# A gated linear attention layer on one Trainium2 core: the scores of each level as pairs of 64 by 64 blocks on the two column halves of TensorE

## The chip, the cores and the metric

The kernel runs on one core of a Trainium2 chip. The metric is the time of one execution in microseconds (us) on the device. Engines are named as the profile names them: PE is TensorE's matmul, PEld its weight load (it overlaps PE), DVE is VectorE, ACT is ScalarE, POOL is GpSimd, SP is SyncE, which issues the DMAs.

## What is computed

One layer of a diffusion backbone: a modulated norm, one input projection of 1024 channels, a bidirectional gated linear attention (4 heads, keys of 128, values of 256), a pooling mixer, two branch projections, a merge by gates, an output projection with residual and final norm, over 1024 latent tokens (256 context tokens give the first states). The part that the change touches is the score term of the attention, in the reference:

```python
diff = b[:, :, :, None, :] - b[:, :, None, :, :]
decay = jnp.exp(jnp.where(tri[:, :, None], diff, -jnp.inf))
scores = jnp.einsum('bhid,bhjd,bhijd->bhij', qc, kc, decay)
o = jnp.einsum('bhij,bhjv->bhiv', scores, vc) + jnp.einsum(
    'bhid,bhdv->bhiv', qc * jnp.exp(b), S)
```

Query i and key j of one chunk meet with a decay per channel, the product of the gates of the tokens between them. Both directions are summed, so a chunk's score matrix A is full, not triangular.

## The kernel before

Inputs, weights and results are float32. The projections split each operand into two float32r parts and add three products (tiles `wh`/`wl` are the parts of a weight, `h` those of the normed input, `ppj` is their PSUM bank, 512 or 256 columns at a time). Attention's own products are plain float32 matmuls, and each of these appears in the trace as two MATMUL records and two weight loads.

The heads run one after the other (`gla(h, ...)`, then `gates`, `head_k`, `head_q` and `head_v` of head h + 1). A head has two halves of 512 tokens, each with four chunks of 128. `head_scores` builds a half's scores in seven levels, for blocks of 1, 2, 4, .. 64 tokens: at a level, each block meets its sibling in a pair of blocks. For a level, `level_scores` multiplies, chunk by chunk, the keys of 128 tokens (`k`, the stationary operand) with the queries of 128 tokens (`level(q, hl)`, the moving one) into the PSUM tile `psc`, and one predicated copy on DVE takes from it, under the level's mask `msk`, what belongs to that level into `A`. Then `double_k` and `double_q` multiply keys (`s2`, `qk`) and queries (the tile `z`, called `qd` in the code) by decays, in place for the queries, which makes them the operands of the next level. So a level is a loop: matmuls, masked copy, decay of queries, matmuls. There are 4 heads x 2 halves x 7 levels = 56 calls.

A tile framework puts the program into an order for each engine ahead of time, by priorities and a cost model, so between the levels' matmuls PE's queue holds projections of the next head or of the pooling branch, and the queue is worked off in that order. In `gates`, matmuls read 64 partitions each (rows 0 to 63 or 64 to 127 of the array; tile `lr`). At the program's start, the modulation vectors are products whose result is 4 rows high (128 x 4 stationary, tiles `sil` and `cs`), which lie on a 32-column strip of the array.

Line numbers: L77 is the helper `mm`, L66 is `tt`, L63 is `act`, L487 the masked copy.

Of the kernel before, what the change touches and what calls it, by code (L numbers as in the profile page):

```python
# [15 lines left out]
P = 128  # L16
# [6 lines left out]
CPH = HALF // P  # L23
# [11 lines left out]

# slots of the one SBUF pool, by tag; PSUM banks, by tag
BUFS = dict(h=32, wr=2, wh=4, wl=4, z=2, t8=1, lr=5, s2=8, sw=2, v=8, qk=8, bx=1, A=2, kt=2, S=6, S0=4, on=1,
# [5 lines left out]
def hybrid_kernel(ctx: ExitStack, tc: tile.TileContext, x, ctx_in, rows, w_mod, b_gate_row,  # L43
# [38 lines left out]
    def split(hi, lo, src):  # L82
        """src = hi + lo, exactly, both float32r"""
        act(hi, src)
        tt(lo, src, hi.bitcast(F32), ALU.subtract)

    def chunks(ap, n=P):
        return ap.rearrange("p (c n) -> p c n", n=n)

    # ---- constants and small vectors as columns  # L90
    cst = const("cst", [P, N_CONST])
# [18 lines left out]

    # ---- token tiles: load, root mean square, normalise
    pow_in = const("pow_in", [P, 10])
# [21 lines left out]

    # ---- low-rank gate inputs, stacked parts on partitions
    def low_rank_weights():
# [16 lines left out]

    # ---- modulation: shift and scale as columns [d, (latent, context)]
    sA = const("sA", [P, KT, 2])
# [7 lines left out]
    def modulate(kt, t0, n, c, ptag):  # L163
        """psum of one row tile of xn^T and the scale and shift that make it h^T"""
        pt = PT(ptag)
        for i in range(n // P):
            nc.tensor.transpose(pt[:, i * P:(i + 1) * P],
                                xs[t0 + i][kt // 4][:, (kt % 4) * P:(kt % 4 + 1) * P], ident)
        return pt[:, :n], sA[:, kt, c:c + 1], shA[:, kt, c:c + 1]
# [71 lines left out]

    # ---- weight stream: slots of 1024 columns, split into exact float32r parts
    ahead = [False]

    def wslot(src, shape, col_scale=None):
        """rows [p, k, n] of a weight; per k: (hi, lo)"""
        _, nk, n = shape
        per = HALF // n
        parts = []
        with tc.high_priority() if ahead[0] else nullcontext():  # L250
            raw = T("wr", shape)
            load(raw, src)
            if col_scale is not None:
                tt(raw, raw, col_scale.rearrange("p (k n) -> p k n", k=1).to_broadcast(shape), ALU.mult)
            for k0 in range(0, nk, per):
                kn = min(per, nk - k0)
                hi, lo = T("wh", [P, kn, n], F32R), T("wl", [P, kn, n], F32R)
                split(hi, lo, raw[:, k0:k0 + kn, :])
                parts += [(hi[:, i, :], lo[:, i, :]) for i in range(kn)]
        return parts  # L260
# [4 lines left out]
    def wquad(w, c0, col_scale=None):  # L265
        """256 columns, all rows"""
        parts = []
        for kh in range(2):
            src = w[kh * HALF:(kh + 1) * HALF, c0:c0 + 256]
            parts += wslot(src.rearrange("(k p) n -> p k n", p=P), [P, 4, 256], col_scale)  # L270
        return parts

    def proj_t(w, rhs_hi, rhs_lo, n):
        """psum[128 columns, n tokens] = W^T h"""
        pt = PT("pj")
        nk = len(w)
        for k in range(nk):
            whi, wlo = w[k]
            mm(pt[:, :n], whi, rhs_hi[k], k == 0, False)
            mm(pt[:, :n], whi, rhs_lo[k], False, False)  # L280
            mm(pt[:, :n], wlo, rhs_hi[k], False, k == nk - 1)
        return pt

    def proj_n(w, lhs_hi, lhs_lo, tok):
        """psum[128 tokens, 256 columns] = h W"""
        pt = PT("pj")
        for k in range(KT):
            whi, wlo = w[k]
            mm(pt[:, :256], lhs_hi[k][:, tok], whi, k == 0, False)
            mm(pt[:, :256], lhs_hi[k][:, tok], wlo, False, False)  # L290
            mm(pt[:, :256], lhs_lo[k][:, tok], whi, False, k == KT - 1)
        return pt
# [25 lines left out]

    # ---- context: final states of both directions
    S0 = [None] * NH  # L320
# [28 lines left out]
    def transpose_k(src, tag):  # L349
        """four of [dk, 128] -> [token, chunk, dk]"""  # L350
        pt = PT("tr")
        for i in range(CPH):
            nc.tensor.transpose(pt[:, i * P:(i + 1) * P], src[i], ident)  # L353
        kT = T(tag, [P, CPH, P])
        act(kT, chunks(pt))
        return kT
# [32 lines left out]

    # ---- latent heads  # L390
    def rope_apply(pt, hf, scale):
# [37 lines left out]

    # Queries and keys lie with their two decays side by side: slot 1 is what a left block gives to the  # L430
    # scores with its right neighbour (backward decay of queries, forward of keys), slot 0 is for right blocks.
    # Decays of tokens and blocks: array 0 has the backward one of the even and the forward one of the odd,
    # array 1 the others.
    DEC_OFF = {2: 0, 4: 256, 8: 384, 16: 448, 32: 480, 64: 496, 128: 504}
# [8 lines left out]
    def level(t, hl):  # L443
        """slot 1 of the even blocks of hl tokens and slot 0 of the odd ones: [pair, block, token]"""
        t = t.rearrange("p n d -> p (n d)").rearrange("p (g x) -> p g x", x=4 * hl)[:, :, 1:4 * hl - 1]
        return t.rearrange("p g (s r) -> p g s r", s=2)[:, :, :, 0:2 * hl - 1:2]

    def gates(h):
        """per half: decays of the tokens, and of the blocks of 2, 4, .. 128 tokens"""
        both = T("bx", [P, 2, 2, HALF])  # L450
# [30 lines left out]
    def level_scores(hl, A, q, k):  # L481
        pl = PT("sc")
        n = P // (2 * hl)
        for c in range(CPH):
            mm(pl[:, c * P:(c + 1) * P], k[:, c * P:(c + 1) * P], level(q, hl)[:, c * n:(c + 1) * n], True, True)
        li = LEVELS.index(hl)
        nc.vector.copy_predicated(A, msk[:, li:li + 1, :].to_broadcast([P, CPH, P]), chunks(pl))  # L487

    def double_q(hl, t, dec):
        """from blocks of hl tokens to blocks of 2 hl"""  # L490
        t = level(t, hl)
        dec = dec.rearrange("p (g s n) -> p g s n", s=2, n=1)[:, :, ::-1, :]
        tt(t, t, dec.to_broadcast([P, HALF // (2 * hl), 2, hl]), ALU.mult)

    def double_k(hl, cur, rest, dec):
        """the same; cur meets its sibling in the scores of a level"""
        shape = [P, HALF // (4 * hl), 2, hl]
# [6 lines left out]
    def head_scores(h, st, decays):  # L504
        """per half: scores within chunks; queries and keys with the decay up to the ends of their chunk:
        qf, qb, kf, kb by chunk; and the decays of the chunks, forward and backward"""
        one, e = decays
# [78 lines left out]

    # ---- context states and latent heads
    msk_f = T("bx", [P, len(LEVELS), P])
# [33 lines left out]

    # ---- pooling branch
    def pool_gate(g):
# [26 lines left out]
    def pool_diff(g, u):  # L651
        """split tiles of (windowed mean - u)^T for one row tile"""
        w = WINDOWS[g]
# [44 lines left out]

    # ---- products of 2 x 2 blocks by seven block products (Winograd's form):
    #      row blocks m of W^T, inner blocks j (odd and even row tiles), token halves hf  # L700
    half_tile = {}

    def slot2(tag, dt=F32R):
        """two tiles of 512 columns"""
        if tag in ("t8", "bx"):
# [17 lines left out]
    def block_operands(o, val):  # L723
        """splits the operands of a row tile pair from the values of R11, R12, R22, R21 (overwritten)"""
        def put(n, v):
# [15 lines left out]
    def operands_h(g, tags, temps):  # L741
        """block operands of h^T, row tiles 2g and 2g + 1"""
        k0, k1 = 2 * g, 2 * g + 1
# [53 lines left out]
    def block_product(w, c0, ops, outs, post, by_rows=False, pre=None):  # L797
        """outs[m][hf] = (W^T X) of two column tiles from c0; post(m, hf) when one is done"""
        with tc.high_priority():
# [46 lines left out]

    # ---- pool groups; block operands of h^T meanwhile
    h_tags = {"T2": ["v"] * 4, "T3": ["lr", "lr", "S0", "S0"], "T1": ["S", "S", "S", "A"], "T4": ["bx", "bx", "kt", "sw"]}
# [53 lines left out]

    # ---- gates of the merge
    def release_order(tags):
# [37 lines left out]
    for i in range(2):  # L942
        for mp in range(4):
            if (i, mp) != (0, 0):
                gate_pair(i, mp)
            if (i, mp) == (1, 1):
                gb_ops.append(gb_operands(0))
    # ---- pool branch output
    gb_ops += [gb_operands(g) for g in range(1, 4)]
# [16 lines left out]

    # ---- attention branch output, merged
    freed = release_order(b_tags)
# [34 lines left out]

    # ---- output projection, residual and final norm
    mH = [[None] * KT for _ in range(2)]
# [107 lines left out]
```

## Time and profile before

| what | value |
|---|---|
| time, median of 3 runs | 1150.31 us (1150.07 to 1152.89) |
| span of the profiled execution | 1152.8 us |
| busy: PE, PEld, DVE, ACT | 1119.6, 926.7, 812.2, 493.4 us |
| chain that ended last: PE's share | 86% |
| TensorE clock granted from 58 us on (mean of the span 0.995) | 1.0 |

The profiled execution's span is the time of the slowest of the three runs less about 0.1 us. Busy times are the sum of an engine's records, and matmul records overlap, so a busy PE says that it was never long without work, not that it ran at its peak. Steps between starts say how long a matmul really holds the engine.

### The profile page before, as it was taken

The page shows a single profiled execution, that of the slowest core. Times are in us where ns is not written, and L with a number is a line of the kernel's source. Part 1 is how long each engine was busy: PE and PEld are TensorE (multiplying, and loading weights), DVE is VectorE, ACT ScalarE, POOL GpSimd, SP SyncE. Part 2 cuts the span into 40 slices and gives each one's busy share as a digit, 9 for nine tenths or more (in the row PEclk, how much of TensorE's full clock was granted, in tenths as well). Part 3 has the DMA queues.
Part 4 walks back from the last instruction along what each step waited for, and adds up shares of the span by engine and source line. Part 5 has one row for each costly group of instructions (what it writes and reads, how often), then busy time and mean ns, then how long its engine had stood idle before and what let it go on. Part 6 is the DMA issues. An engine that isn't in the chain of part 4 may idle for free.

```text
span 1152.8 us, 16292 instructions
## 1 busy us (share of the span) xinstructions
PE 1119.6 (97%) x5993; PEld 926.7 (80%) x5993; DVE 812.2 (70%) x1533; ACT 493.4 (43%) x962; POOL 24.2 (2%) x50
## 2 busy tenths in 40 slices
PE   6799999999999999999999999999999999999997
PEld 1268998798798798788888888888887886878997
DVE  4677458488588587698988867665768776757454
ACT  6697552462452552543333433343446324113233
POOL 0100000000000000100000000000000000000001
PEclk9899999999999999999999999999999999999999
DMA  8812150120220310103251463524448468982113
GB/s 292 291 37 74 42 151 28 56 73 20 65 65 20 85 44 20 55 28 119 82 161 50 128 201 119 167 84 129 151 137 269 161 197 287 298 302 94 38 38 146
DMA packets 119660, 138.40 MB, mean 120 GB/s; under 512 B 8803, under 2 KB 80669, under 8 KB 119454
## 3 DMA queue, kind: packets, MB, share of 16 engines
q1 hardware_dynamic: 119582, 137.38, 37.6%
q8 instruction: 47, 0.77, 0.3%
q14 instruction: 31, 0.25, 0.1%
HBM read 100.65 MB, written 32.51 MB: 116 GB/s over the span
## 4 chain that ended last, share of the span: by engine, by line
PE 86%; DMA 6%; ACT 2%; DVE 2%; issue 2%; SPq 1%; POOL 1%; POOLq 0%; ACTq 0%; DVEq 0%
PE ppj L77 59%; PE psc L77 19%; PE pst L77 3%; PE po L77 2%; DMA h<-w_mod 1%; DMA qk<-ga 1%; PE ptr L77 1%; DMA qk<-x 1%; DMA qk<-gb_T 1%; DMA wr<-w_in 1%; PE ptr L353 1%; ACT sw L63 1%; SPq L80 1%; DMA wr<-w_b 0%; DMA S<-ctx 0%
## 5 line engine op out<-in xcount | busy, mean ns | idle before, releaser
L77 PE MATMUL ppj<-h,wh 128*128 128x512 f32 x794 | 257.9, 401 | 1.0 <-ACT h L63 1.0
L63 ACT ACTIVATE wh<-wr 128x512 fp32r<-128x512 f32 (+1 forms) x183 | 113.7, 627 | 189.9 <-PE ppj L77 108.0
L77 PEld LDWEIGHTS ppj<-h,wh 128*128 128x128 f32 x794 | 146.8, 188 | 35.1 <-issue 2.9
L66 DVE TENSOR_TENSOR wl<-wr,wh 128x512 fp32r<-128x512 f32 (+1 forms) x183 | 124.8, 686 | 61.2 <-ACT wh L63 56.2
L77 PE MATMUL ppj<-wh,h 128*128 128x256 f32 x800 | 157.7, 283 | 0.0
L77 PE MATMUL ppj<-h,wl 128*128 128x512 f32 x397 | 157.2, 396 | 0.0
L77 PEld LDWEIGHTS ppj<-wh,h 128*128 128x128 f32 x800 | 129.9, 190 | 0.5 <-ACT qk L63 0.4
L77 PE MATMUL ppj<-wl,h 128*128 128x256 f32 x400 | 113.2, 283 | 0.0
L77 PEld LDWEIGHTS ppj<-h,wl 128*128 128x128 f32 x397 | 74.6, 188 | 15.1
L77 PEld LDWEIGHTS ppj<-wl,h 128*128 128x128 f32 x400 | 76.0, 190 | 0.2
L77 PEld LDWEIGHTS psc<-z,s 128*128 128x128 f32 x384 | 48.1, 188 | 9.8 <-issue 7.6
L487 DVE COPY_PREDICATED A<-msk,psc 128x512 f32<-128x512 uint8 x56 | 41.2, 735 | 19.8 <-PE psc L77 19.7
L77 PE MATMUL psc<-z,s 128*128 128x128 f32 x384 | 53.5, 280 | 0.0
L63 ACT ACTIVATE s<-s 128x512 f32<-128x512 f32 x60 | 36.9, 629 | 36.7 <-DVE s L66 31.6
L66 DVE TENSOR_TENSOR s<-s,ppj 128x512 f32<-128x512 f32 x60 | 40.7, 683 | 17.0 <-PE ppj L77 17.0
L63 ACT ACTIVATE s<-qk 128x256 f32<-128x256 f32 x56 | 23.1, 420 | 59.8 <-DVE qk L66 59.8
L74 DVE SCALAR_TENSOR_TENSOR S<-S,dec,pst 128x256 f32<-128x256 f32 x56 | 26.8, 478 | 26.3 <-PE pst L77 26.0
L77 PE MATMUL ppj<-S,wh 128*128 128x512 f32 (+1 forms) x132 | 41.2, 371 | 0.0
L77 PE MATMUL psc<-h,wh 128*128 128x512 f32 x126 | 39.1, 392 | 0.0
L66 DVE TENSOR_TENSOR s<-s,psc 128x512 f32<-128x512 f32 x43 | 29.2, 683 | 11.9 <-PE psc L77 10.2
L66 DVE TENSOR_TENSOR s<-s,bx 128x256 f32<-128x256 f32 (+1 forms) x64 | 30.5, 487 | 7.5 <-ACT bx L63 7.5
L66 DVE TENSOR_TENSOR on<-wr,wr 128x512 f32<-128x512 f32 x21 | 14.5, 691 | 30.0 <-DMA wr<-w_in 24.2
(518 smaller groups left out, 2390.3 us busy)
## 6 DMA issues: line engine op xcount, KB each, us to landing
wr<-w_in SPq DMA_DIRECT2D x65, 512.0 KB, 3.9
h<-w_mod SPq DMA_DIRECT2D x32, 256.0 KB, 5.4
qk<-sg SPq DMA_DIRECT2D x32, 256.0 KB, 5.3
sg<-s SPq DMA_DIRECT2D x28, 256.0 KB, 2.1
sw<-qk SPq DMA_DIRECT2D x64, 64.0 KB, 2.0
gb_T<-qk SPq DMA_DIRECT2D x16, 256.0 KB, 3.6
qk<-o SPq DMA_DIRECT2D x16, 256.0 KB, 4.7
ga<-s SPq DMA_DIRECT2D x16, 256.0 KB, 2.2
```

The source lines that it names most:

```text
L63: return nc.scalar.activation(out, in_, func, **kw)
L66: return nc.vector.tensor_tensor(out=out, in0=a, in1=b, op=op)
L74: return nc.vector.scalar_tensor_tensor(out=out, in0=a, scalar=s, in1=b, op0=op0, op1=op1)
L77: return nc.tensor.matmul(out, lhsT=lhsT, rhs=rhs, start=start, stop=stop)
L80: return nc.sync.dma_start(out=out, in_=in_)
L353: nc.tensor.transpose(pt[:, i * P:(i + 1) * P], src[i], ident)
L487: nc.vector.copy_predicated(A, msk[:, li:li + 1, :].to_broadcast([P, CPH, P]), chunks(pl))
```

## The change

Of the 128 by 128 product of a chunk at a level, only two 64 by 64 blocks are wanted: for blocks up to 32 tokens the two on the diagonal, for blocks of 64 tokens the two off it. Now each is a matmul of its own: 64 columns of keys are stationary, 64 queries move. The first block goes to PSUM partitions 0 to 63, so to array columns 0 to 63, the second to partitions and columns 64 to 127. The masked copy becomes two, of 64 partitions by 4 x 64 elements. Comments were also removed, which moves line numbers by a few.

```diff
 def level_scores(hl, A, q, k):
     pl = PT("sc")
-    n = P // (2 * hl)
+    n, hc = P // (2 * hl), P // 2
     for c in range(CPH):
-        mm(pl[:, c * P:(c + 1) * P], k[:, c * P:(c + 1) * P], level(q, hl)[:, c * n:(c + 1) * n], True, True)
+        for r in range(2):
+            cols_, k0 = (c * P + (1 - r if hl == hc else r) * hc), c * P + r * hc
+            ql = level(q, hl)
+            ql = ql[:, c:c + 1, 1 - r, :] if hl == hc else ql[:, c * n + r * n // 2:c * n + (r + 1) * n // 2]
+            mm(pl[r * hc:(r + 1) * hc, cols_:cols_ + hc], k[:, k0:k0 + hc], ql, True, True)
     li = LEVELS.index(hl)
-    nc.vector.copy_predicated(A, msk[:, li:li + 1, :].to_broadcast([P, CPH, P]), chunks(pl))
+    for r in range(2):
+        rs, o = slice(r * hc, (r + 1) * hc), (1 - r if hl == hc else r) * hc
+        nc.vector.copy_predicated(A[rs, :, o:o + hc], msk[rs, li:li + 1, o:o + hc].to_broadcast([hc, CPH, hc]),
+                                  chunks(pl)[rs, :, o:o + hc])
```

The order of the engines shifts with it. PE's queue in the first half of head 0, from the second to the third level, before (`psc` with `z` and `s2` is a level's block, `ppj` the projection of the next head's keys):

```order
L77 MATMUL psc_362_1811<-z_359_1797,s2_361_1806 128x128 x4
L77 MATMUL ppj_435_2178<-h_57_264,wl_432_2171 128x512
L77 MATMUL ppj_435_2178<-h_61_275,wh_431_2170 128x512
L77 MATMUL ppj_435_2178<-h_62_276,wh_431_2170 128x512
L77 MATMUL ppj_435_2178<-h_61_275,wl_432_2171 128x512
L77 MATMUL ppj_435_2178<-h_122_492,wh_433_2174 128x512
L77 MATMUL ppj_435_2178<-h_123_493,wh_433_2174 128x512
L77 MATMUL ppj_435_2178<-h_122_492,wl_434_2175 128x512
L77 MATMUL psc_364_1822<-z_359_1797,s2_363_1817 128x128 x4
```

And after, at the same place:

```order
L77 MATMUL psc_362_1816<-z_359_1797,s2_361_1811 64x64 x8
L77 MATMUL ppj_435_2248<-h_61_275,wh_431_2240 128x512
L77 MATMUL ppj_435_2248<-h_62_276,wh_431_2240 128x512
L77 MATMUL ppj_435_2248<-h_61_275,wl_432_2241 128x512
L77 MATMUL ppj_435_2248<-h_122_492,wh_433_2244 128x512
L77 MATMUL ppj_435_2248<-h_123_493,wh_433_2244 128x512
L77 MATMUL ppj_435_2248<-h_122_492,wl_434_2245 128x512
L77 MATMUL ppj_435_2248<-h_126_503,wh_433_2244 128x512
L77 MATMUL ppj_435_2248<-h_127_504,wh_433_2244 128x512
L77 MATMUL ppj_435_2248<-h_126_503,wl_434_2245 128x512
L77 MATMUL psc_364_1832<-z_359_1797,s2_363_1827 64x64 x8
```

Eight matmuls of 64 by 64 stand where four of 128 by 128 stood, each block's between projections that use the whole array, and nine projections lie between these two blocks where seven did. Over the two halves of head 0, 102 matmuls of other work lie between blocks where 90 did (8.2 to a gap before, 9.3 now); they are taken forward from those that follow the scores, and their number in all is the same. Of the 57 pieces in which the blocks lie, the change leaves 57 (one block, at the first level of head 0, lies in two pieces before and after).

DVE's queue in the first half of head 0, before, from the fourth masked copy:

```order
L487 COPY_PREDICATED A_1790<-msk,psc_1833 128x512
L66 TENSOR_TENSOR z_1797<-z_1797,bx_1009 128x32x2x8
L66 TENSOR_TENSOR qk_892<-s_371_1861,bx_1009 128x2x128
L66 TENSOR_TENSOR s_381_1906<-s_379_1895,bx_1009 128x64x2x2
L487 COPY_PREDICATED A_1790<-msk,psc_1844 128x512
```

And after, at the same place:

```order
L493 COPY_PREDICATED A_1790<-msk,psc_1848 64x4x64 x2
L66 TENSOR_TENSOR z_1797<-z_1797,bx_1009 128x32x2x8
L66 TENSOR_TENSOR s_373_1907<-s_371_1891,bx_1009 128x2x2x64
L66 TENSOR_TENSOR qk_892<-s_371_1891,bx_1009 128x2x128
L66 TENSOR_TENSOR s_379_1935<-qk_857,s_242_1026 128x128x2
L493 COPY_PREDICATED A_1790<-msk,psc_1864 64x4x64 x2
```

Both masked copies of a level stand ahead of the decay of the queries (`z<-z,bx`), for which the next level's matmuls wait, as the one copy did.

The gates' matmuls, which the prediction uses as a measure, stand in PE's queue so before the change (before head 0; `psc_240` and `psc_241` are the two directions, of array rows 0 to 63 and 64 to 127, and `lr_71` and `lr_72` the two parts of the weight):

```order
L77 MATMUL psc_240_1012<-lr_205_755,lr_71_311 128x512
L77 MATMUL psc_240_1012<-lr_205_755,lr_72_312 128x512
L77 MATMUL psc_241_1019<-lr_205_755,lr_71_311 128x512
L77 MATMUL psc_241_1019<-lr_205_755,lr_72_312 128x512
L77 MATMUL po_244_1028<-lr_141_557,lr_71_311 128x512
L77 MATMUL po_244_1028<-lr_141_557,lr_72_312 128x512
```

Two matmuls of the upper rows stand ahead of two of the lower ones; the change does not move them against each other here.

## Rows read from the trace of the kernel before

**Rows 1.** The page: span, busy times, the chain by engine and by line

```profile
span 1152.8 us, 16292 instructions
PE 1119.6 (97%) x5993; PEld 926.7 (80%) x5993; DVE 812.2 (70%) x1533; ACT 493.4 (43%) x962; POOL 24.2 (2%) x50
...
PE 86%; DMA 6%; ACT 2%; DVE 2%; issue 2%; SPq 1%; POOL 1%; POOLq 0%; ACTq 0%; DVEq 0%
```

**Rows 2.** Busy time of each engine in the score and filler stretches of heads 1, 2

```profile
core 0: us, PE busy (x) PEld busy (x) DVE busy (x) ACT busy (x) POOL busy (x), PEclk, DMA share, GB/s
...
253.00:292.00 39.00, 39.00 (x243) 33.28 (x243) 33.22 (x67) 11.86 (x25) 0.00 (x0) 1.00 0.15 41
292.00:337.00 45.00, 44.41 (x280) 38.50 (x279) 27.64 (x75) 26.57 (x57) 2.76 (x4) 1.00 0.22 60
```

**Rows 3.** Groups by line and shape, whole span (busy us, mean ns, idle before)

```profile
L77 PE MATMUL psc<-z,s 128*128 128x128 f32 x384 | 53.5, 280 | 0.0
...
L487 DVE COPY_PREDICATED A<-msk,psc 128x512 f32<-128x512 uint8 x56 | 41.2, 735 | 19.8 <-PE psc L77 19.7
```

**Rows 4.** Timeline of one level's block, PEld alone (start, duration, count, idle before)

```profile
176.56 0.19 PEld L77 LDWEIGHTS ppj<-h,wl 128*128 128x128 f32 x1
177.02 0.98 PEld L77 LDWEIGHTS psc<-z,s 128*128 128x128 f32 x8 [0.28 <-issue]
177.93 0.30 PEld L77 LDWEIGHTS ppj<-h,wh 128*128 128x128 f32 x2
```

**Rows 5.** Waits of the score stretch of head 1 (total us, times, longest)

```profile
DVE A L487 <- PE psc L77: 4.6, 7, 1.0
...
PEld psc L77 <- issue: 2.0, 8, 0.4
...
PEld psc L77 <- DVE z L66: 0.3, 1, 0.3
```

**Rows 6.** Timeline of the gates' matmuls before head 0, PE alone

```profile
103.97 0.62 PE L77 MATMUL ppj<-h,wh 128*128 128x512 f32 x2
104.42 0.39 PE L77 MATMUL ppj<-h,wl 128*128 128x512 f32 x1
104.74 0.73 PE L77 MATMUL psc<-lr,lr 64*128 64x512 f32 x4
105.31 0.62 PE L77 MATMUL po<-lr,lr 64*128 64x512 f32 x2
```

**Rows 7.** The same stretch, PEld alone

```profile
104.74 0.30 PEld L77 LDWEIGHTS psc<-lr,lr 64*128 64x128 f32 x4 [0.35 <-issue]
105.08 0.42 PEld L77 LDWEIGHTS po<-lr,lr 64*128 64x128 f32 x2
105.86 0.19 PEld L77 LDWEIGHTS ppj<-wh,h 128*128 128x128 f32 x1 [0.36 <-ACT qk L63]
105.97 0.19 PEld L77 LDWEIGHTS ppj<-wl,h 128*128 128x128 f32 x1
```

**Rows 8.** Timeline at the start: full array, then a 32-column strip

```profile
32.26 0.84 PE L77 MATMUL ppj<-h,z 128*128 128x512 f32 x3
...
33.03 0.09 PEld L77 LDWEIGHTS ptr<-h,sil 128*4 128x4 f32 x2 [0.35 <-issue]
33.03 1.02 PE L77 MATMUL ptr<-h,sil 128*4 128x512 f32 x2
```

**Rows 9.** Timeline of DVE over one level of head 1

```profile
259.24 0.73 DVE L487 COPY_PREDICATED A<-msk,psc 128x512 f32<-128x512 uint8 x1
259.86 0.68 DVE L66 TENSOR_TENSOR z<-z,bx 128x512 f32<-128x512 f32 x1
260.45 0.42 DVE L66 TENSOR_TENSOR qk<-s,bx 128x256 f32<-128x256 f32 x1
260.79 0.42 DVE L66 TENSOR_TENSOR s<-s,bx 128x256 f32<-128x256 f32 x1
...
262.04 0.73 DVE L487 COPY_PREDICATED A<-msk,psc 128x512 f32<-128x512 uint8 x1
```

## The prediction

> **What bounds the kernel now.** I read the page first: PE is busy for 97% of the 1152.8 us and makes 86% of the chain that ended last [rows 1]. So the question is only how long PE's queue takes, unless something else comes to the front. The stretches come next: while a head's scores run, PE is busy in all of 39.00 us and DVE in 33.22; in the stretch behind it, PE in 44.41 of 45.00 and DVE in 27.64 [rows 2]. DVE is the engine to watch, and only in the score stretches. Then the groups: the levels' matmuls have a mean record of 280 ns [rows 3], but records overlap, so I take steps between starts. In one level's block, eight weight loads (each with its matmul) take 0.98 us from the first start to the last end; less the last one's 0.19 that is seven steps, so 0.113 us a step, and the next projection's load stands at 177.93, eight steps behind the first one [rows 4]. A block so holds PE for 8 x 0.113 = 0.90 us. To this comes what stands ahead of the first load: in this block it began at 177.02, with 0.28 of idle time ahead of it, so it was not fetched ahead, and its 0.11 us lay open. Eight of the 14 blocks of head 1 had such an opening [rows 5]; 8/14 x 0.11 is 0.06, and a little real waiting for DVE comes to it (0.3 us in 14 blocks, the same rows). I take 0.97 us a block, and 57 pieces x 0.97 = 55 us of PE's time for all levels.
>
> **The matmuls after.** What a matmul costs by its columns: two plain float32 records of 512 columns span 1.02 us where two of 512 on float32r span 0.62 [rows 6, 8]. In the second case a record is 0.39 and the step so 0.23: a record outlasts its step by 0.16. With the same tail the first case is twice the step and 0.16, so 0.43 us for 512 columns, 0.107 for 128. The measured 0.113 is that and 0.006 of handling. With 64 columns: 0.053 + 0.006 = 0.059 us. The weight load has the same size: two loads 0.11 apart in an idle array (105.86 and 105.97, [rows 7]) carry 128 columns, so 64 take 0.055 and hide behind a matmul of 0.059.
>
> So a level has 16 steps of 0.059 us = 0.944 in place of 8 of 0.113 = 0.904. By itself the change gains nothing: all hangs on whether the two column halves run at the same time, and on what it costs to cut the array and to join it again.
>
> Both have a near relative in the trace. The gates use two row halves of the array. Four of their 512-column matmuls span 0.73 us [rows 6]. In a line they would span 3 x 0.23 + 0.39 = 1.08; two and two they span one load of 0.11, one step of 0.23 and a record of 0.39, which is 0.73. So two halves of the array do run side by side, weight loads too: four loads span 0.30 us, where two in a line span 0.30 already [rows 7]. These were halves of rows, not of columns; no row shows two column strips at once. I take the nearest relative: side by side.
>
> The price of cutting stands in the same rows. The last matmul on the whole array starts at 104.42 and streams for 0.23, to 104.65; the first load on halves comes at 104.74, 0.09 later. The way back: the last one on halves starts at 105.54 (105.31 + 0.62 - 0.39), streams to 105.77, and the load for the whole array comes at 105.86: 0.09 again [rows 6, 7]. At a column strip it is the same: the last of three full-array matmuls starts at 32.71 (32.26 + 0.84 - 0.39), streams to 32.94, and the strip's load stands at 33.03 [rows 8]. So each switch empties the array for 0.09 us and leaves the next load uncovered.
>
> The block after, then: 0.09 (empty) + 0.055 (first load of 64 columns) + 8 x 0.059 = 0.47 (two halves, eight steps each) + 0.09 (empty) + 0.107 (first load of 128 columns) = 0.81 us, against 0.97. That is -0.16 us a piece, 57 x 0.156 = **-8.9 us**. The one block that lies in two pieces pays its switch pair once more with little saved: +0.3. Bounds: with no handling time, eight steps of 0.053, -11.5; with 0.065 a step, -6.2.
>
> How the matmuls leave the queue decides a part of this. In the gates' order, two matmuls of the upper rows stand ahead of two of the lower ones, and since two of one half can't share it, the pairs that ran together were first and third, second and fourth: a half did not wait for its neighbour's turn [rows 6]. The sum above goes by this row. The Trainium skill (TensorE: Matmul & The Clock Gate, Part 3: Packing small matmuls — row/col tiling) says otherwise: matmuls start and end strictly in the order of the program. By that rule a second half would start only with the first half's second record, and the gain would be the smaller one of rival 2.
>
> **The masked copies.** DVE's copy of 4 x 128 elements holds it for 0.62 us (259.24 to 259.86); of plain operations, 512 elements take 0.59 (259.86 to 260.45) and 256 take 0.34 (260.45 to 260.79) [rows 9]. Half the elements so save 0.25 and the rest is fixed: a copy of 64 partitions and 256 elements is 0.37, if partitions don't count, and the two are 0.74, +0.12 us a level, 56 x 0.12 = 6.7 us in all. Bounds: 0 (if the fixed part overlaps) and 0.21 (if nothing does: a record of 0.73 less 0.26 is 0.47, twice that less 0.73). They lie in the loop of a level: matmuls, copies, decay of the queries, next matmuls. The loop's matmuls get shorter by as much or more (0.90 to 0.6 from first load to last step), so the loop as such is no longer than it was. DVE's amount is the second question: in the score stretch it has 5.8 us free in 39 [rows 2] and needs 14 x 0.12 = 1.7 more. The cover is projections: 9.3 matmuls of other work now lie between two blocks where 8.2 did, +0.25 us of work for PE, twice what DVE needs. Half of the copies waited for PE anyway (7 of 14, [rows 5]); at the other half DVE is the late one, as in rows 9, where it has next to no gap over a level. I charge less than half of 28 x 0.12 = 3.4 us: **+1.5 us** of new waiting of PE. Without the cover it would be 6.7.
>
> **Sum.** -8.9 + 0.3 + 1.5 = -7.1 us. The profiled execution's 1152.8 would be 1145.7. It was the slowest of three and stands 2.5 above their median, so against 1150.3 I predict **1143.3 us**.
>
> **Rivals.**
> 1. The halves do not overlap (slower). Then a block is 0.09 + 0.055 + 16 x 0.059 + 0.09 + 0.107 = 1.29 us, +0.32 each, 57 x 0.32 + 0.3 = +18.3: 1168.6. With 0.053 a step, +13: 1163. For it: both column halves take their operands from the same 128 partitions, where the gates' row halves take them from different ones. Against it: the pair in [rows 6]. It decides where a block's 16 take over 0.65 us from the first load to the last step: with half an overlap the change is worth nothing. The same page of the Trainium skill (Measured speedup vs the span model) has three column strips 2.38 times as fast as in a line; no row here shows that.
> 2. Side by side, but strictly in order. A chunk's four records then take two steps, 0.118, so four chunks and a last step 0.53, a block 0.87, 57 x 0.097 = -5.5, with the rest -3.7: 1146.6.
> 3. DVE takes the gain. If the score stretches come to be DVE's, +6.7 and more stand against -8.6: 1148 to 1151. For it: rows 9. Against: 5.8 us free in each stretch.
> 4. Cutting by columns empties the array for longer than by rows. At 0.18 a switch instead of 0.09, the gain is gone; with 0.25, +11: 1161. The single strip in [rows 8] speaks against it.
>
> **How the numbers follow.** Forecast 0.42; rival 1 0.22; rival 2 0.18; rival 3 0.12; rival 4 0.06. A measurement of this kernel can tell about 0.3% (3.5 us) from no change. Faster by more: the forecast and most of rival 2 (0.14), 0.56. Within: the rest of rival 2, nearly all of rival 3, 0.15. Slower: rivals 1 and 4 and the worst of 3, 0.29. The forecast's own range is 1139 to 1147. For eight in ten the range must reach into rival 1, of which it takes the cheap end: 1138 to 1164; above it lies some 0.15.
>
> **What would show it.** Right: two records of 64 by 64 start within a few ns of each other, on both halves; the 16 loads of a block span about 0.6 us, not 1.0; the load behind a block stands 0.09 after its stream's end; masked copies are x112 at about 0.47 us; PE's idle time ahead of a block hardly grows. Wrong: steps of 0.06 one behind the other over all 16 (rival 1), or PE waiting for the decay of the queries at most levels (rival 3).

## The result: 1158.4 us, slower, and the profile after

The changed kernel takes 1158.39 us (median of 4, 1157.45 to 1159.36), the kernel before 1150.22 on the same chip (median of 4). The ratio is 1.0063, with an interval of 1.0043 to 1.0083: slower, by 7.2 us at this ratio (8.2 between the medians), where 7 us less were forecast. The profiled execution took 1157.71 us.

The two profiled executions lie closer together than that. In every run where both are known, the time lies 1.7 to 2.2 us above the span (here 1157.71 and 1155.9). By that, the profiled execution of before, with its span of 1152.8, took some 1154.6 us and is none of the listed runs; that it was the slowest of them, as is said ahead of the prediction and in it, does not fit. The forecast rests on differences and does not hang on this. The two traces differ by 3.1 us in all: 5.1 more from the first level's block to the end, and 2.0 less ahead of it, where both kernels have the same 858 matmul records (why is not shown; the mean granted clock up to 58 us is 0.92 in before and 0.95 in after).

The page of after (span, busy times, the chain by engine, the masked copies):

```profile
span 1155.9 us, 17232 instructions
...
PE 1113.2 (96%) x6441; PEld 908.2 (79%) x6441; DVE 829.2 (72%) x1589; ACT 494.4 (43%) x962; POOL 25.4 (2%) x50
...
PE 73%; DVE 11%; DMA 7%; ACT 4%; issue 3%; POOL 1%; SPq 1%; POOLq 0%; DVEq 0%; ACTq 0%
...
L493 DVE COPY_PREDICATED A<-msk,psc 64x256 f32<-64x256 uint8 x112 | 49.7, 444 | 7.7 <-PE psc L77 5.6
```

Against [rows 1], PE is busy for 6 us less and DVE for 17 more, and DVE's share of the chain that ended last went from 2% to 11%. Against [rows 3], DVE no longer stands idle for 20 us ahead of the masked copies, but for 8, and 5.6 of these are waits for PE: DVE has more often become the later one.

The same two stretches as in [rows 2], busy time by engine:

```profile
core 0: us, PE busy (x) PEld busy (x) DVE busy (x) ACT busy (x) POOL busy (x), PEclk, DMA share, GB/s
253.00:292.00 39.00, 38.44 (x347) 29.11 (x342) 36.42 (x80) 11.39 (x24) 0.00 (x0) 1.00 0.14 41
292.00:337.00 45.00, 43.35 (x290) 37.86 (x289) 27.76 (x75) 26.82 (x58) 3.14 (x4) 1.00 0.22 59
```

DVE's free time in the score stretch went from 5.8 us to 2.6; PE is idle for longer in both stretches, 0.6 and 1.6 us.

A level's block in after, weight loads alone (the counterpart of [rows 4]):

```profile
259.11 0.55 PEld L77 LDWEIGHTS psc<-z,s 128*64 128x64 f32 x16 [0.36 <-issue]
259.73 0.19 PEld L77 LDWEIGHTS ppj<-h,wl 128*128 128x128 f32 x1
```

From the block's first load to the next projection's are 0.62 us: a load of 0.055, eight steps of 0.059 and 0.09 of emptying make 0.617. The single records say the same: matmuls start at 259.113 and 259.120, then at 259.223 and 259.230, 259.281 and 259.288, and so on to 259.576 and 259.583, on the two halves 7 ns apart.

DVE in after over three levels (start, duration, count), the counterpart of [rows 9]:

```profile
265.12 0.69 DVE L66 TENSOR_TENSOR wl<-wr,wh 128x512 fp32r<-128x512 f32 x1
265.84 0.92 DVE L493 COPY_PREDICATED A<-msk,psc 64x256 f32<-64x256 uint8 x2
266.80 0.69 DVE L66 TENSOR_TENSOR z<-z,bx 128x512 f32<-128x512 f32 x1
267.40 0.42 DVE L66 TENSOR_TENSOR s<-qk,s 128x256 f32<-128x256 f32 x1
267.86 0.48 DVE L74 SCALAR_TENSOR_TENSOR S<-S,dec,pst 128x256 f32<-128x256 f32 x1
268.26 0.42 DVE L66 TENSOR_TENSOR s<-s,bx 128x256 f32<-128x256 f32 x1
268.59 0.90 DVE L493 COPY_PREDICATED A<-msk,psc 64x256 f32<-64x256 uint8 x2
269.50 0.69 DVE L66 TENSOR_TENSOR z<-z,bx 128x512 f32<-128x512 f32 x1
```

Two things are to be read here. A pair of copies holds DVE from 265.84 to 266.80, 0.96 us; over all levels the mean is 0.940, where the one copy before held it 0.629. And ends and starts: `s` at 267.40 starts 0.09 ahead of the end of `z` (266.80 + 0.69), as DVE's operations do throughout [rows 9]; but `z` starts 0.04 *behind* the end of the copies (265.84 + 0.92).

The score stretch of head 1 from the first to the last start of its levels' matmuls, before:

```profile
L77 PE MATMUL psc<-z,s x96: 273/275/372, 257.9 to 291.4; 128*128 128x128 f32 x96
...
L77 PE MATMUL psc<-z,qk x16: 274/274/382, 254.9 to 274.4; 128*128 128x128 f32 x16
```

and after:

```profile
L77 PE MATMUL psc<-z,s x192: 218/220/272, 256.2 to 290.7; 128*64 128x64 f32 x192
...
L77 PE MATMUL psc<-z,qk x32: 218/220/273, 252.4 to 273.3; 128*64 128x64 f32 x32
```

36.5 us became 38.3, although the blocks in it got shorter. Over four heads the score stretches took 8.3 us more, the three gaps between them 5.4 less (projections had moved from there into the scores), and the part behind the last one 2.2 more.

### The profile page after: what moved, and what is told of

Read it like the earlier page. It is cut to its first block, busy times and chain, and to the rows that moved or that the text cites. A ratio compares the mean times of both kernels' runs of the same rounds, so it can differ in the third digit from the quotient of the medians.

```text
span 1155.9 us, 17232 instructions
## 1 busy us (share of the span) xinstructions
PE 1113.2 (96%) x6441; PEld 908.2 (79%) x6441; DVE 829.2 (72%) x1589; ACT 494.4 (43%) x962; POOL 25.4 (2%) x50
## 4 chain that ended last, share of the span: by engine, by line
PE 73%; DVE 11%; DMA 7%; ACT 4%; issue 3%; POOL 1%; SPq 1%; POOLq 0%; DVEq 0%; ACTq 0%
PE ppj L77 49%; PE psc L77 17%; PE pst L77 3%; PE po L77 2%; DVE wl L66 2%; DMA h<-w_mod 1%; DVE s L66 1%; ACT bx L63 1%; DVE bx L66 1%; DMA qk<-ga 1%; PE ptr L77 1%; DVE z L66 1%; DMA qk<-x 1%; DMA wr<-w_in 1%; DMA qk<-gb_T 1%
## 5 line engine op out<-in xcount | busy, mean ns | idle before, releaser
L493 DVE COPY_PREDICATED A<-msk,psc 64x256 f32<-64x256 uint8 x112 | 49.7, 444 | 7.7 <-PE psc L77 5.6
L77 PEld LDWEIGHTS psc<-z,s 128*64 128x64 f32 x768 | 26.8, 136 | 20.7 <-issue 17.3
L77 PE MATMUL psc<-z,s 128*64 128x64 f32 x768 | 33.0, 226 | 3.4 <-DVE z L66 2.9
L77 PE MATMUL ppj<-v,wh 128*128 128x512 f32 (+1 forms) x116 | 35.2, 361 | 0.0
```

What stands on the lines that cost most here:

```text
L77: return nc.tensor.matmul(out, lhsT=lhsT, rhs=rhs, start=start, stop=stop)
L493: nc.vector.copy_predicated(A[rs, :, o:o + hc], msk[rs, li:li + 1, o:o + hc].to_broadcast([hc, CPH, hc]), chunks(pl)[rs, :, o:o + hc])
```

## What the experiments tell apart

The kernel before ran anew beside each group of experiments, at 1153.0 to 1154.3 us, so ratios are compared, not times.

**1. Two copies on the matmuls of before.** Only the copy is changed:

```diff
-        nc.vector.copy_predicated(A, msk[:, li:li + 1, :].to_broadcast([P, CPH, P]), chunks(pl))
+        hc = P // 2
+        for r in range(2):
+            rs, o = slice(r * hc, (r + 1) * hc), (1 - r if hl == hc else r) * hc
+            nc.vector.copy_predicated(A[rs, :, o:o + hc], msk[rs, li:li + 1, o:o + hc].to_broadcast([hc, CPH, hc]),
+                                      chunks(pl)[rs, :, o:o + hc])
```

> The kernel before with its 128 by 128 matmuls, and the masked copy in the two parts of the change. Theory A: DVE pays 56 x 0.31 = 17.7 us more and PE saves nothing, so 1158 to 1168. Theory B: nearly nothing changes for PE, 1150 to 1153.

Measured: 1171.48 us, ratio 1.0148 (1.0128 to 1.0168), +17.1 us. DVE's timeline:

```profile
259.53 0.90 DVE L490 COPY_PREDICATED A<-msk,psc 64x256 f32<-64x256 uint8 x2
260.44 0.69 DVE L66 TENSOR_TENSOR z<-z,s 128x512 f32<-128x512 f32 x1
```

A pair holds DVE for 0.91 us here too, 0.931 in the mean. With 56 x (0.931 - 0.629) = 16.9 us more on DVE, the time grew by 17.1. The copies alone are dearer than the whole change: 1.0148 against 1.0063 is 9.8 us, which the matmuls, and the other order of the queues that came with them, gave back.

**2. One copy fewer.** The change with the copy of the upper 64 partitions alone:

```diff
         li = LEVELS.index(hl)
-        for r in range(2):
+        for r in range(1):
```

> This kernel leaves out the masked copy of the lower 64 partitions, so half of the scores of every level is missing; the matmuls are those of the change. Theory A (the change's two masked copies hold DVE 0.94 us a level instead of 0.63, and PE waits for the decay of the queries behind them): with one copy of 0.48 left, DVE is freer than before the change and PE keeps its gain of 0.16 us a block: 1138 to 1144 us. Theory B (what was lost comes with the cut array and the other order of PE's queue, not from DVE): 1154 to 1159, as the change.

Measured: 1148.74 us, ratio 0.9945 (0.9925 to 0.9964). Half of each level's scores is left out. The one copy holds DVE for 0.34 us:

```profile
258.40 0.44 DVE L493 COPY_PREDICATED A<-msk,psc 64x256 f32<-64x256 uint8 x1 [0.42 <-PE psc L77]
258.74 0.68 DVE L66 TENSOR_TENSOR z<-z,bx 128x512 f32<-128x512 f32 x1
```

With cheap copies the new matmuls gain. One reservation: each kernel gets its own order from the framework. Here 92 matmul records of other work lie in the score stretch of head 1; in the change 124, in before 110, in experiment 1 113. So experiment 1 is close to a price of the copies alone, and this one is not.

**3. Two copies by chunks on the matmuls of before.** Is it that there are two instructions?

```diff
-        nc.vector.copy_predicated(A, msk[:, li:li + 1, :].to_broadcast([P, CPH, P]), chunks(pl))
+        for i in range(2):
+            cc = slice(2 * i, 2 * i + 2)
+            nc.vector.copy_predicated(A[:, cc], msk[:, li:li + 1, :].to_broadcast([P, 2, P]), chunks(pl)[:, cc])
```

> The kernel before with the masked copy in two parts of 128 partitions by 2 chunks (the same 256 elements a partition as a half copy of the change). If the price comes of half the partitions, the parts overlap like whole copies do, 0.37 us each, +0.12 a level: 1150 to 1156. If it comes of two masked copies in a row, or of 256 elements being dear, the pair takes 0.94 as in the change, and the time is that of the kernel before with two half copies. Theory B: 1150 to 1153.

Measured: 1153.45 us, ratio 0.9996 (0.9981 to 1.001).

```profile
260.36 0.77 DVE L489 COPY_PREDICATED A<-msk,psc 128x256 f32<-128x256 uint8 x2
261.02 0.68 DVE L66 TENSOR_TENSOR z<-z,bx 128x512 f32<-128x512 f32 x1
```

The same number of elements by instruction, all 128 partitions: the pair holds DVE for 0.66 us (0.670 in the mean), not 0.94. So neither the second instruction nor 256 elements are dear (0.04 us a level); the partitions are. This run and experiment 1 also have nearly the same order: 5953 of the 5993 matmul records stand in the same sequence, and 1580 of DVE's 1589 operations. So 1.0148 against 0.9996, 17.5 us, is the price of the two ranges of partitions and hardly one of another order.

**4. Both blocks at one place.** The diagonal products too are made of 64 by 64 blocks, and both blocks of a chunk lie at the same 64 columns of PSUM, so that one copy of 128 partitions by 256 elements takes both. ACT moves the last level and the lower diagonal blocks to their place.

```diff
+    def pair_scores(pt, q_of, k):
+        for c in range(CPH):
+            for r in range(2):
+                k0 = c * P + r * HC
+                mm(pt[r * HC:(r + 1) * HC, c * HC:(c + 1) * HC], k[:, k0:k0 + HC], q_of(c, r), True, True)
+        return chunks(pt[:, :CPH * HC], HC)
...
+        if hl == HC:
+            pl = pair_scores(PT("sc"), lambda c, r: ql[:, c:c + 1, 1 - r, :], k)
+            act(A[:HC, :, HC:], pl[:HC])
+            act(A[HC:, :, HC:], A[HC:, :, :HC])
+            act(A[HC:, :, :HC], pl[HC:])
+            return
...
+        nc.vector.copy_predicated(A[:, :, :HC], msk[:, li:li + 1, :].to_broadcast([P, CPH, HC]), pl)
```

> The matmuls of the change, also for the products on the diagonal, with both blocks of a chunk at the same 64 columns of PSUM, so that one masked copy of 128 partitions by 256 elements takes a level into the left half of each chunk's columns; the last level and the move of the lower diagonal blocks to their place are three copies on ACT per half. Theory A: DVE needs about 0.4 us a level instead of 0.63 before and 0.94 in the change, PE keeps its gain: 1134 to 1142, faster than before. Theory B: 1150 or more.

Measured: 1143.61 us, ratio 0.9907 (0.989 to 0.9923): 10.7 us faster than before, and faster than both kernels.

```profile
261.23 0.45 DVE L502 COPY_PREDICATED A<-msk,psc 128x256 f32<-128x256 uint8 x1 [0.17 <-PE psc L77]
261.56 0.68 DVE L66 TENSOR_TENSOR z<-z,bx 128x512 f32<-128x512 f32 x1
```

The copy holds DVE for 0.33 us, and DVE waits for PE again ahead of it. There are 48 masked copies instead of 56, since ACT takes the last level.

**5. That version with every masked copy issued twice.** Did it win by its matmuls or by its cheaper copy?

```diff
+        for _ in range(2):
+            nc.vector.copy_predicated(A[:, :, :HC], msk[:, li:li + 1, :].to_broadcast([P, CPH, HC]), pl)
```

> Both blocks at one place, as in the faster kernel, but with each level's one masked copy issued twice (the second changes nothing), so that DVE's masked copies take 0.67 us a level, close to the 0.63 of the kernel before, on full partitions. If the matmuls on the column halves are worth what their shorter blocks say, and DVE at its load of before holds nobody up, 0.989 to 0.995 of the kernel before. If the faster kernel gained by DVE's relief alone, 0.998 to 1.003.

Measured: 1149.97 us, ratio 0.9962 (0.9946 to 0.9979), just above the band that was expected. Each copy holds DVE for 0.34 us, so with DVE's copies at about the load of before, some 4 us of gain remain; about 6 of experiment 4's go with the lighter copy, though the two kernels differ a little in the order of their queues too.

**6. Are the copies dear because they stand in the level's loop?** The change, with the copies behind the decays:

```diff
-                level_scores(hl, A, qd, ck)
-                ck = double_k(hl, ck, k, dec[0])
+                masked_copy = level_scores(hl, A, qd, ck)
                 double_q(hl, qd, dec[1])
+                ck = double_k(hl, ck, k, dec[0])
+                masked_copy()
```

> The change, with the decay of the queries issued ahead of the two masked copies, so that the next level's matmuls no longer wait for the copies; DVE's amount of work stays. Theory L (the copies cost because they lie in the loop of a level, between its matmuls and the next ones): they come out of it, and the time is 1140 to 1148, faster than the kernel before. Theory M (DVE's amount decides: 0.94 instead of 0.63 us a level, whatever the order): 1155 to 1162, as the change.

Measured: 1172.17 us, ratio 1.016 (1.0141 to 1.0179). The gain of theory L did not come, and the time lies above theory M's range too. The score stretches did get shorter (34.0 to 36.3 us, in after 38.3 to 39.8), but the gaps between them grew to 49.9 to 53.3 (45.1 to 45.4) and the part behind the last from 696.3 to 707.3. The order of the queues changed with the move, so this run does not decide between the two theories.

**7. The same move on the kernel before**, as a control.

> The kernel before with its one masked copy behind the decay of the queries, as a control for the order alone. Both theories: PE waited little for DVE before, so within 0.3% of the kernel before; if it gains more than that, the order of PE's queue is worth something by itself, which would have to be taken off the gain of the run with the change's copies last.

Measured: 1160.82 us, ratio 1.0059 (1.0042 to 1.0077). Its score stretch of head 1:

```profile
L77 PE MATMUL psc<-z,s x96: 273/275/381, 257.1 to 284.0; 128*128 128x128 f32 x96
...
L77 PE MATMUL psc<-z,qk x16: 273/274/353, 255.2 to 270.9; 128*128 128x128 f32 x16
```

28.8 us where before has 36.5, and still slower: the next head's first block came 56.6 us behind the last one here, 47.2 in before, so from head to head 85.4 against 83.7. A score stretch is short when few projections lie in it. Its length alone says nothing.

**8. The same move on experiment 4** (the diff of 6; at the last level ACT's three moves go back with it).

> Both blocks of a chunk at one place of PSUM and one masked copy of 128 partitions by 256 elements, issued behind the decay of the queries. There PE was already kept waiting little. Theory L: 0 to 4 us below the same kernel with the copy first (ratio to the kernel before 0.987 to 0.991). Theory M: no change against it, ratio 0.989 to 0.992.

Measured: 1146.57 us, ratio 0.9935 (0.9913 to 0.9957); score stretches of 26.7 us, 30.9 in experiment 4, and no gain.

**9. The lower copy alone.** The counterpart of experiment 2:

```diff
         li = LEVELS.index(hl)
-        for r in range(2):
+        for r in range(1, 2):
```

> The change without the masked copy of the upper 64 partitions (it leaves out half of each level's scores): the mirror of the run that kept only the upper copy, where a copy held DVE for 0.34 us. If a step of DVE from one start partition to another costs its overlap, this copy starts late behind an operation of all partitions and the next one late behind it, and it holds DVE for about 0.48 us. If 64 partitions or the second copy in a row are the reason, it is 0.34 as in the mirror.

Measured: 1151.43 us (one run). All queues have the order of experiment 2, which had 1148.74.

```profile
257.99 0.42 DVE L66 TENSOR_TENSOR s<-s,bx 128x256 f32<-128x256 f32 x1
258.44 0.45 DVE L493 COPY_PREDICATED A<-msk,psc 64x256 f32<-64x256 uint8 x1
258.92 0.69 DVE L66 TENSOR_TENSOR z<-z,bx 128x512 f32<-128x512 f32 x1
```

The same elements as the upper copy, but it starts 0.03 us behind the end of `s` and `z` 0.03 behind its own: it holds DVE for 0.48 us, not 0.34, and begins later.

**10. The lower copy in two.** The change, the second copy cut by chunks into two of 64 partitions:

```diff
-        for r in range(2):
+        for r, cc in ((0, slice(0, CPH)), (1, slice(0, 2)), (1, slice(2, CPH))):
```

> The change with the lower half's masked copy cut once more, into two of 64 partitions by 2 chunks (128 elements), so that two copies of the lower 64 partitions follow each other. If an operation loses its overlap only where the start partition changes (upper to lower, lower to all), the first lower copy hands over to the second after about 0.2 us (0.34 less 128 elements at 0.27 us for 256). If operations on the lower half never overlap, it is 0.33 or more.

Measured: 1167.7 us (one run).

```profile
259.80 0.98 DVE L493 COPY_PREDICATED A<-msk,psc 64x256 f32<-64x256 uint8 x3
260.81 0.69 DVE L66 TENSOR_TENSOR z<-z,bx 128x512 f32<-128x512 f32 x1
```

Of the single records, 54 second lower copies that follow a lower copy all start 0.09 us ahead of its end; of the lower copies behind an operation that begins at partition 0 (53 behind the upper copy, 5 behind one of all partitions), 58 of 58 start 0.01 to 0.03 behind its end. 64 partitions are not what hinders the overlap, a change of the first partition is.

**11. The change once more.**

> The change itself, once more, beside the run with the doubled copy and on the same chip: 1.004 to 1.009 of the kernel before if the first measurement holds.

Measured: 1160.17 us, ratio 1.006 (1.004 to 1.0081): the result stands.

**12. The lower copy first.** The change with its copies exchanged; all else keeps its place in the queues:

```diff
         li = LEVELS.index(hl)
-        for r in range(2):
+        for r in (1, 0):
```

> The change with its two masked copies in the other order, the lower 64 partitions first. Two theories of when a DVE operation loses its overlap with the one before it. N: when its tiles begin at another partition than those of its neighbour ahead. H: when an input begins at another partition than the input that DVE last read from the same memory (SBUF or PSUM), or its output at another than the last output there, whichever operation that was. In the change N lets two starts a level come late (lower copy, decay of the queries); H also an upper copy or another operation that reads PSUM as the first one behind a lower copy, and the trace of the change has 44 of these, 21 upper copies and 23 full-width ones. Here, by N and by H, the late ones are the lower copy (0.03 us behind the end of its predecessor) and the upper copy behind it, and the decay of the queries starts some 0.08 before the end of the upper copy. By N the count per level is the same as in the change, and so the time: 1.006 of the time before. By H the 44 are gone, no full-width operation starts late, 44 x 0.115 = 5 us of DVE are saved, and where DVE is what the loop waits for, about half or all of it comes back: 1.002 to 1.004 of the time before.

Measured: 1159.94 us, ratio 1.005 (1.0033 to 1.0067).

```profile
259.42 0.41 DVE L66 TENSOR_TENSOR s<-s,bx 128x256 f32<-128x256 f32 x1
259.86 0.90 DVE L493 COPY_PREDICATED A<-msk,psc 64x256 f32<-64x256 uint8 x2
260.66 0.67 DVE L66 TENSOR_TENSOR z<-z,bx 128x512 f32<-128x512 f32 x1
```

The starts are those of theory H: the lower copy is late (259.42 + 0.41 is 259.83), and `z` now starts 0.10 ahead of the copies' end. Of the full-width operations that theory H calls late, 2 are left, where the change has 79, and all of these do start late. By the rule, 88 operations in all start late here, 156 in the change. The time is not what H expected: the score stretches are shorter by only 0.3 to 0.5 us each, 1.6 in all, for these 68 late starts, and the part behind the last took 702.0 us, 5.7 more than in the profile of the change, with the same order of instructions on every engine. The ratio lies above the band given for H and can't be told from the change's.

## Why the prediction was wrong, point by point

**The matmuls after: right.** The block was to take 0.81 us with its two switches; 0.62 from its first load to the next one, the 0.09 ahead of it and the next load's 0.107 make 0.82. Rival 1 (16 steps in a line, 0.944 us) and rival 4 (a dearer switch) are out. Rival 2's strict order would make it 0.055 + 0.53 + 0.09 = 0.675 from the first load to the next projection's, where 0.62 stand. The order in the trace is the one of [rows 6], the halves in pairs, and not the strict one by records that rival 2 took. The Trainium skill (TensorE: Matmul & The Clock Gate, Part 3: Packing small matmuls — row/col tiling) has matmuls start and end in the order of the program. The block itself does not decide on this: counted by whole matmuls, each of two records, its starts would fit. The gates do, since a matmul is one record there: they start at 104.738, 104.745, 105.075 and 105.080, in two pairs, where two matmuls of the upper rows ahead of two of the lower ones could form a pair only in the middle under that rule. On this point the measured starts decide against the Trainium skill.

PE's own sum was right too. From every step between two starts I took what that matmul takes when nothing is late (0.227 us for 512 columns on float32r, 0.43 in float32, 0.113 for 128, 0.059 for a pair of 64). From the first block to the end this gives -24.2 us of streaming (56 x (0.904 - 0.472)) and +15.9 of switches and uncovered loads (57 x 0.345, less 3.8 of uncovered loads before): -8.3, forecast -8.9 + 0.3. The rest are PE's waits, against before, worked out in the same way:

| waits of PE more than before, us | in the scores | between heads | behind the last | sum |
|---|---|---|---|---|
| the change | 2.7 | 4.8 | 5.8 | 13.3 |
| two copies, matmuls of before (1) | 12.1 | 4.3 | 2.7 | 19.1 |
| the change, upper copy alone (2) | -2.0 | 4.4 | 3.2 | 5.6 |
| the change, lower copy first (12) | 1.2 | 4.8 | 11.4 | 17.4 |

-8.3 + 13.3 is +5.0, and the stretch from the first block to the end went from 983.2 to 988.3. So the sum fell at its smallest term, the +1.5 us of waiting.

Not all in the column behind the last stretch is waiting. After 58 us, before's trace has the granted clock at 1.0 up to its last 2 us; in the change's it falls to the lower of its two levels (1.2 of 2.4 GHz) once more, and matmuls of 512 columns take 0.43 us a step there, not 0.23. That is 1.6 of the change's 5.8 us, and in the other rows 3.3, 1.5 and 2.9. The mean clock of before's own runs varies from 0.988 to 0.996, so this is in part chance. The line (columns as in the stretches of the result; 0.50 is the granted clock):

```profile
543.60:547.00 3.40, 3.40 (x10) 2.65 (x9) 2.91 (x5) 1.15 (x2) 0.00 (x0) 0.50 0.00 0
```

**The step that failed: "The masked copies".** It priced a copy at 0.37 us "if partitions don't count" and the pair at +0.12 a level, with 0.21 as the bound. It measured +0.311, outside both bounds: 17.4 us of DVE, not 6.7. One slip is in the upper bound itself. For a pair without any overlap it took twice 0.47, and these 0.94 us are what was measured; but it subtracted the old copy's whole record of 0.73 from them, and not the 0.62 for which that copy held DVE. From start to start the bound is 0.32, and 56 x 0.32 is 17.9 us. The other error is the choice of the low value, by which each copy lets the next operation start ahead of its end, as in [rows 9]. The number of elements was priced well enough (the upper copy alone holds 0.34 us, experiment 2). Partitions do count, not by their number but by where they begin. In [rows 9] each operation starts some 0.08 us ahead of the end of the one before. In the change, an operation does not if its tile begins at another partition than the last one in that memory: it starts about 0.03 behind the end, some 0.11 us later. Behind a masked copy it is more: in experiment 3, operations start 0.107 ahead of a masked copy's end, and here 0.025 behind it, so 0.13 later. The lower copy (from partition 64) and `z` behind it (from 0) both pay this, 0.26 us of the 0.311; 0.04 are the second instruction (experiment 3), and 0.01 is left.

Which tile counts shows in three more places of after's timeline above. The upper copy at 265.84 is late (`wl` ends at 265.81), though it and `wl` both begin at partition 0: the last tile that DVE read from PSUM, with four operations in between, was a lower copy's. The sum `S` at 267.86, which reads PSUM (`pst`) as the first one behind a lower copy, is late too. And the upper copy at 268.59, which has `S` between it and the last lower copy, starts 0.09 ahead of the end of its predecessor. Sorted by this rule, over the whole span of after: 156 operations that follow another within 0.06 us have an operand of this kind, and none of them overlaps its predecessor; of the 1091 others 989 do. 44 of the 156 lie outside the pairs (21 upper copies, 23 operations of all partitions), another 5 us of DVE. In before there is none with such an operand. Experiment 12 moved the late starts as the rule says. The Trainium skill states this rule, as a model (VectorE: DVE Perf Modes, Two Vector instructions with no wait between them: an instruction is held until all earlier ones are done if an input starts in another group of 32 partitions than the last input read from that memory, or an output in another than the last output there). The trace agrees in every one of these cases; the Trainium skill gives no duration there, which here is 0.11 to 0.13 us. The prediction missed a rule that was written down.

**"The loop as such is no longer than it was", and the cover.** The loop's matmuls did get shorter by 0.3 us, but its copies longer by as much. A score stretch wanted 14 x 0.311 = 4.4 us more of DVE, and of the 5.8 that were free 2.6 are left. The projections taken forward did cover this: PE's waits in the scores grew by 2.7 us in all, where the same copies without as much cover cost 12.1 (table, second row). But the cover was not free, as the prediction had it: the waits came behind the scores instead, +4.8 us between heads. There, from 292 to 337 us, the largest are matmuls into `po` that wait for ACT's `on`: 1.2 us on PE and 1.8 on its weight loads, 0.6 before. Over the whole gap, in before's order PE waits 2.8 to 2.9 us, in the change's 4.2 to 4.7. That is not a matter of the copies alone: with one cheap copy (2) it is 4.2 to 4.4, and in the control (7), with fewer projections in the scores, 4.3 to 4.5. Any other order of this queue that I ran waits longer there than before's. The control's 0.6% is what such a change of order can cost by itself.

**Rival 3 came nearest,** "DVE takes the gain", with too low a price: with 17.4 in place of 6.7 its own sum is 1150.3 - 8.6 + 17.4 = 1159.1. That this meets the measured 1158.4 is in part luck, since PE waits only 2.7 us more in the score stretches themselves and the rest elsewhere (table). What the runs show is the price of the copies: +17.1 us alone (1), where two copies of all partitions cost nothing (3), and a gain with the new matmuls once a level has one cheap copy (2 and 4). The -9.8 us that remain for the new matmuls is the difference of two ratios, not a measurement of its own.

**What stays open.** How much of the 13.3 us belongs to the copies and how much to the changed order: the copies' part is 7.7 by the third row of the table (13.3 - 5.6), but that kernel has an order of its own. One piece of the order can be placed. At 542.9 us, in the pooling branch, PE waits 2.57 us for ACT's `t`; in before it does not wait there. ACT's queue before:

```profile
537.86 0.58 ACT L63 ACTIVATE t<-psc 128x512 f32<-128x512 f32 x1
540.52 0.63 ACT L63 ACTIVATE h<-on 128x512 fp32r<-128x512 f32 x1 [2.08 <-DVE on L66]
```

and after, with PE's wait:

```profile
540.59 0.63 ACT L63 ACTIVATE h<-on 128x512 fp32r<-128x512 f32 x1 [3.59 <-DVE on L66]
542.26 0.58 ACT L63 ACTIVATE t<-psc 128x512 f32<-128x512 f32 x1
542.90 0.73 PE L77 MATMUL psc<-bx,wh 128*128 128x512 f32 x2 [2.57 <-ACT t L63]
```

In the change `t` stands behind `h`, which waits for DVE's `on`, and that in turn for a DMA; in before, and in experiments 1, 2, 4, 5 and 7, it stands ahead, and PE does not wait there. The fall of the clock shown above follows right behind this wait. The wait and the fall make 4.2 of the 5.8 us behind the last stretch, in a part that no masked copy lies in; they come with the order that the framework chose here. Experiment 6 has another order again, and a wait of 6.7 us at this place. Experiment 12 took 5.7 us more than the change behind the last stretch: PE waits there 0.9 us more for this `t`, 1.5 more at 893 us (2.19 against 0.69) and 1.7 more at 969 us, and the clock falls a second time, 1.3 us more. Why the same order waits longer in one run than in another is not shown.

## What to carry to other kernels

When products are packed onto parts of the array, look first at who takes the results away: two operations on two ranges of partitions held DVE 50% longer here than one over all, while the two results at the same columns of PSUM could be taken by one (experiment 4, 1143.6 us). Price an operation on DVE by what stands before it too, from start to start, and ask for each where its tiles begin. In a queue whose order is fixed ahead, work taken forward as a cover is missing later: count the stretch that it comes from, and look for new waits also where the change has no work.

## What the runs showed of the hardware that was not expected

A change of the first partition costs DVE its overlap, 0.11 to 0.13 us at each late start, and it is remembered for each memory, over operations in between. A wait of PE can cost more than itself: behind 2.57 us of waiting at 542.9 the granted clock fell to the lower level, and 1.6 us more were lost; a wait of 2.3 us in before, at 889 us, was followed by no such fall. And, expected but not on any row of before: two column halves of the array, fed from the same 128 partitions, ran side by side with their weight loads, 7 ns apart, at 0.059 us for a pair of 64 by 64 float32 steps.
